# Spreading a per-token factor over all partitions: through DRAM, or with a product of ones on the matmul engine

## The chip, the cores and the metric

One core of a Trainium2 chip runs the whole program in one launch. The engines work in order, each through its own list of instructions, and wait for one another by semaphores: PE multiplies matrices (PEld is its weight load), DVE and ACT work on vectors, POOL does a little, and SP issues all transfers between DRAM and the on-chip memory. On-chip memory has 128 partitions; results of PE land in banks of a second memory (PSUM) of 128 partitions by 512 words. The metric is the device time of one execution in microseconds (us), lower is better.

## The reference, cut to what matters

```python
def rmsnorm(x, w):                       # x: (1, 512, 1024)
    xf = x.astype(jnp.float32)
    y = xf * lax.rsqrt(jnp.mean(xf * xf, axis=-1, keepdims=True) + EPS)
    return (y * w.astype(jnp.float32)).astype(x.dtype)

def hybrid_layer(x, layer_idx, norm_w, w_in, ...):
    h = rmsnorm(x, norm_w)
    proj = jnp.einsum('bsd,de->bse', h, w_in)      # 1024 -> 4608 columns
    aq, ak, av, ag, bq, bk, bv, bg, cu, cg = jnp.split(proj, splits, axis=-1)
    ...                                            # attention, retention, pooling, gates
    mixed = jnp.concatenate([o_a, o_b, o_c], axis=-1)
    return x + jnp.einsum('bse,ed->bsd', mixed, w_out)

def reference(...):                                # two layers, then a last rmsnorm
    h = x
    for l in range(DEPTH):
        h = hybrid_layer(h, l, ...)
    return rmsnorm(h, final_norm_w)
```

512 tokens of 1024 values pass through two layers. The factor of this text is the `lax.rsqrt(...)` of the first rmsnorm: one number for each token, 512 in all.

## The kernel before, in words

All matrices are float32. Each is split into a high and a low half that PE can multiply (`split`, line 449: ACT writes the high half, DVE the rest), and a product of two such matrices is three products (`mm3`, line 495): high by high, high by low, low by high. Names: hh and hl are the halves of the normalised input, stored transposed (channels on partitions); wh and wl those of a block of weights, 128x1024 words, 512 KB, loaded into wraw. Five pairs wh/wl exist and two buffers wraw, so a load may start when both halves of the block two places earlier have been written. In this text the blocks are numbered from 0: blocks 0 to 3 are the value columns bv, block 4 is cg0, block 5 cu0, block 6 cu1.

In the first layer the input arrives transposed from the host. hh and hl there hold x times the norm's weight without the factor of its token, so that PE need not wait for the factors, and each result is multiplied by the factors afterwards. Where tokens lie on partitions (the values, `store_values`, line 739) the factor of a partition is enough: it stands in the four columns `self.rc` (part of the tile edge, 128x4; column t holds tokens 128t to 128t+127). Where tokens lie along the free axis (gates, pooling, rotated q and k), every partition needs all 512 factors in a row: `self.rb`, 128x512. DVE multiplies with it (`scaled_T` line 748, `c_pool` line 906, the tables cos and sin line 777).

The step R of START (lines 730 to 733) makes rb from rc through DRAM: it writes the four columns as a row of 512 words, each word apart, and reads that row back into all 128 partitions.

```python
row = nc.tile("dram", "row", [S], 4, F32)
nc.sync.dma_start(row.rearrange("(t p) -> p t", t=NT), self.rc)
nc.sync.dma_start(self.rb, row.partition_broadcast(P))
```

The order of instructions isn't that of the code. A recorder takes down all operations; a planner (`Recorder.schedule`, line 220) then goes through them with its own model of costs and latencies (`cost`, line 323, and LATENCY) and priorities (place in the program less a boost by kind, HIGH), and writes one list for each engine. Tiles of one tag share a few buffers, granted in the order in which the program names them: 4 of "soft" (128x512), 4 of "T", 1 of "u", 2 banks "tp", 3 banks "pj". Units follow ORDERS: for layer 0 "bv t0 t1 cg0 cu0 cu1 bg0 bg1 bqk0 B0 ..."; t0 (`decay_tables`, line 580) makes small tables out of a load of 8x2 words, in a buffer "soft", by a chain of tiny DVE steps and one exponential on ACT.

Of the kernel before, what the change touches and what calls it, by code (L numbers as in the profile page):

```python
# [9 lines left out]
F32 = mybir.dt.float32  # L10
F32R = mybir.dt.float32r
AF = mybir.ActivationFunctionType
ALU = mybir.AluOpType
AX = mybir.AxisListType

P = 128
S = 512
D = 1024
KD = D // P
NT = S // P  # L20
# [7 lines left out]
UW = PADL + S + 8  # L28
# [341 lines left out]
def record(ins: dict, out: bass.AP):  # L370
    nc = Recorder()
    x_d = ins["x"][0]

    def sb(tag, shape, bufs=1, dt=F32, name=None):
        return nc.tile("sb", tag, shape, bufs, dt)

    def bank(tag, bufs):
        return nc.tile("psum", tag, [P, S], bufs, F32)

    def pj():  # L380
        return bank("pj", 3)

    def lgp():
        return bank("lg", 2)

    def tpp():
        return bank("tp", 2)

    def ovp():
        return bank("ov", 1)  # L390

    def soft():
        return sb("soft", [P, S], 4)

    def ttile(shape=(P, 1024), dt=F32):
        return sb("T", shape, 4, dt)
# [12 lines left out]
    def load_x(t):  # L409
        for half in range(2):  # L410
            nc.sync.dma_start(xt[t][half], x_d[t * P:(t + 1) * P, HALF[half]])
# [2 lines left out]
    nc.vector.memset(neghalf, -0.5)  # L414
    nc.scalar.copy(sb("st", [P, 4], 4), neghalf)
    ident = sb("ident", [P, P])


    granules = [(i, shape) for i, (_, _, _, shape) in enumerate(weight_granules())]
# [3 lines left out]
    def emit_granule(parts=1):  # L423
        at, (nk, nc_) = granules[len(wt)]
        shp = [P, nk, nc_]
        src = ins["wg"][at].rearrange("p (k c) -> p k c", k=nk)
        raw = sb("wraw", shp, 2)
        hi = sb("wh", shp, WBUFS, F32R)
        lo = sb("wl", shp, WBUFS, F32R)
        n = shp[1] // parts  # L430
        for i in range(parts):
            k = slice(i * n, (i + 1) * n)
            was, nc.boost = nc.boost, HIGH.get("w", 0)
            nc.sync.dma_start(raw[:, k, :], src[:, k, :])
            split(hi[:, k, :], lo[:, k, :], raw[:, k, :])
            nc.boost = was
        wt.append((hi, lo))
# [11 lines left out]
    def split(dh, dl, src):  # L449
        nc.scalar.copy(dh, src)  # L450
        nc.vector.tensor_tensor(dl, src, dh.bitcast(F32), op=ALU.subtract)
# [3 lines left out]
    def square(t, half, junk, part=None):  # L455

        if half == 0:
            stats[t] = sb("st", [P, 4], 4)
        st = stats[t]
        c = slice(0, 512) if part is None else part  # L460
        at = half if c.stop == 512 else 3
        nc.scalar.activation(junk, xt[t][half][:, c], AF.Square, scale=1.0 / math.sqrt(D), accum_out=st[:, at:at + 1])
        if half == 0:
            nc.vector.tensor_scalar(st[:, 0:1], st[:, 0:1], EPS, None, op0=ALU.add)
        elif c.stop < 512:
            nc.vector.tensor_tensor(st[:, 0:1], st[:, 0:1], st[:, 3:4], op=ALU.add)
        else:
            nc.vector.tensor_scalar(st[:, 1:2], st[:, 1:2], st[:, 0:1], None, op0=ALU.add)
            nc.gpsimd.tensor_tensor(st[:, 2:3], st[:, 1:2], neghalf[:, 0:1], op=ALU.pow)
# [25 lines left out]
    def mm3(ps, lh, ll, rh, rl, first, last):  # L495
        nc.tensor.matmul(ps, lh, rh, start=first, stop=False)
        nc.tensor.matmul(ps, lh, rl, start=False, stop=False)
        nc.tensor.matmul(ps, ll, rh, start=False, stop=last)
# [180 lines left out]
    class Layer:  # L679
# [18 lines left out]
        def first_values(self):  # L698

            self.vh, self.vl = sb("vh", [P, NT, 512], 1, F32R), sb("vl", [P, NT, 512], 1, F32R)  # L700
            self.rb, self.rc = sb("rb", [P, S]), edge[:, 28:32]

            dummy = sb("soft", [P, S], 4, mybir.dt.bfloat16)
            nc.vector.memset(dummy, 0.0)
            warm = tpp()
            for _ in range(WARM):
                nc.tensor.matmul(warm[:, 0:256], dummy[:, 0:P], dummy[:, 0:256], start=True, stop=True)
            banks = [lgp(), lgp(), ovp(), pj()]
            for u in START.split():
                i = int(u[1:] or 0)  # L710
                if u[0] == "k":
                    xw = ttile()
                    nc.sync.dma_start(xw[:, 0:S + 4], ins["xT_w"][i * P:(i + 1) * P, :])
                    raw, w = xw[:, 0:S], xw[:, S:S + 1]
                    nc.scalar.activation(self.hh[:, i, :], raw, AF.Copy, scale=w)
                    nc.vector.scalar_tensor_tensor(self.hl[:, i, :], raw, w, self.hh[:, i, :].bitcast(F32), op0=ALU.mult, op1=ALU.subtract)
                    if i % 2 == 0:
                        emit_granule(2 if i < FINE else 1)
                    wh, wl = wt[i // 2]
                    for t in range(NT):  # L720
                        ts = slice(t * P, (t + 1) * P)
                        mm3(banks[t], self.hh[:, i, ts], self.hl[:, i, ts], wh[:, i % 2, :], wl[:, i % 2, :], i == 0, i == KD - 1)
                elif u[0] == "x":
                    load_x(i)
                    for half in range(2):
                        square(i, half, soft())
                    nc.vector.tensor_copy(self.rc[:, i:i + 1], stats[i][:, 2:3])
                elif u[0] == "I":
                    nc.sync.dma_start(ident, ins["c_ident"])
                elif u[0] == "R":  # L730
                    row = nc.tile("dram", "row", [S], 4, F32)
                    nc.sync.dma_start(row.rearrange("(t p) -> p t", t=NT), self.rc)
                    nc.sync.dma_start(self.rb, row.partition_broadcast(P))
                else:
                    for t in range(NT):
                        self.store_values(t, banks[t])
            wstate[0] = 4
# [291 lines left out]
@with_exitstack  # L1029
def trunk(ctx: ExitStack, tc: tile.TileContext, ins: dict, out: bass.AP):  # L1030
    pools = {
        "sb": ctx.enter_context(tc.tile_pool(name="sb", bufs=1)),
        "psum": ctx.enter_context(tc.tile_pool(name="ps", bufs=1, space=bass.MemoryType.PSUM)),
        "dram": ctx.enter_context(tc.tile_pool(name="dr", bufs=1, space=bass.MemoryType.DRAM)),
    }
    with tc.manual_schedule():
        for op in record(ins, out).schedule():
            for b in op.bases:
                if b.real is None:
                    name = f"{b.tag}_{b.slot}"  # L1040
                    b.real = pools[b.space].tile(b.shape, b.dt, tag=name, bufs=1, name=name)

            def real(v):
                return v.resolve() if isinstance(v, View) else v

            name, method = op.method
            op.inst = getattr(getattr(tc.nc, name), method)(*[real(a) for a in op.args], **{k: real(v) for k, v in op.kw.items()})  # L1047
# [67 lines left out]
```

## Time and profile before

| | |
|---|---|
| runs, us | 682.93, 682.99, 681.54; median 682.93 |
| profiled execution | 682.16 us, its span 680.4 us |
| busy share | PE 97%, PEld 80%, DVE 74%, ACT 52%, POOL 4% |
| DMA | 71.86 MB, mean 106 GB/s |
| first real product of PE | at 4.78 us, behind the cast of a weight block |
| granted clock, 30 to 55 us in steps of 5 | 1.00, 0.63, 0.50, 0.85, 1.00 |

Times in the profile count from the span's start. A row of a timeline is an instruction or several alike, with its start, its duration, and in brackets the idle time of its engine before it and what ended that. SPq is SP's queue of transfers; its rows show when a transfer is issued, not when it has landed. PEclk is the clock that PE was granted, 1.00 for 2.4 GHz and 0.50 for 1.2 GHz. Matmuls overlap, so the time of one in a stream is the distance of two starts, not the duration shown. All the kernel's own instructions carry line 1047, from where they are issued; the tile names tell them apart.

### The profile page before, as it was taken

The page shows a single profiled execution, that of the slowest core. Times are in us where ns is not written, and L with a number is a line of the kernel's source. Part 1 is how long each engine was busy: PE and PEld are TensorE (multiplying, and loading weights), DVE is VectorE, ACT ScalarE, POOL GpSimd, SP SyncE. Part 2 cuts the span into 40 slices and gives each one's busy share as a digit, 9 for nine tenths or more (in the row PEclk, how much of TensorE's full clock was granted, in tenths as well). Part 3 has the DMA queues.
Part 4 walks back from the last instruction along what each step waited for, and adds up shares of the span by engine and source line. Part 5 has one row for each costly group of instructions (what it writes and reads, how often), then busy time and mean ns, then how long its engine had stood idle before and what let it go on. Part 6 is the DMA issues. An engine that isn't in the chain of part 4 may idle for free. (4 is left out here: it accounts for less than half of the span.)

```text
span 680.4 us, 8912 instructions
## 1 busy us (share of the span) xinstructions
PE 660.3 (97%) x3171; PEld 541.3 (80%) x3171; DVE 500.3 (74%) x954; ACT 354.0 (52%) x701; POOL 30.3 (4%) x51
## 2 busy tenths in 40 slices
PE   9959999999999999999999999899999999999996
PEld 6747887888788888887888888688888887888785
DVE  4558988787787998976574778767568857887733
ACT  6524683534376866553443766344437765665321
POOL 0000000000000000001010000000000000000011
PEclk9969999999999999999999999999999999999999
DMA  8436434422225223243312423532331143124302
GB/s 309 163 123 187 141 93 125 124 93 78 87 61 171 77 91 104 72 116 95 107 63 78 139 68 85 139 109 73 104 118 59 62 137 107 61 92 97 92 31 93
DMA packets 29973, 71.86 MB, mean 106 GB/s; under 512 B 6004, under 2 KB 10260, under 8 KB 29928
## 3 DMA queue, kind: packets, MB, share of 16 engines
q1 hardware_dynamic: 29928, 71.29, 34.4%
q8 instruction: 25, 0.41, 0.3%
q14 instruction: 20, 0.16, 0.1%
HBM read 69.09 MB, written 2.18 MB: 105 GB/s over the span
## 5 line engine op out<-in xcount | busy, mean ns | idle before, releaser
L1047 PE MATMUL pj<-hh,wh 128*128 128x512 f32 x448 | 178.5, 400 | 8.7 <-ACT wh L1047 7.2
L1047 PE MATMUL pj<-hl,wh 128*128 128x512 f32 x448 | 177.8, 397 | 0.0
L1047 PE MATMUL pj<-hh,wl 128*128 128x512 f32 x448 | 177.2, 397 | 0.0
L1047 ACT CAST wh<-wraw 128x1024 fp32r<-128x1024 f32 (+1 forms) x97 | 100.8, 1039 | 108.5 <-PE pj L1047 73.9
L1047 DVE TENSOR_TENSOR wl<-wraw,wh 128x1024 fp32r<-128x1024 f32 (+1 forms) x97 | 117.3, 1209 | 28.5 <-ACT wh L1047 28.0
L1047 PEld LDWEIGHTS pj<-hh,wh 128*128 128x128 f32 x448 | 84.9, 190 | 27.8 <-ACT wh L1047 7.6
L1047 PEld LDWEIGHTS pj<-hh,wl 128*128 128x128 f32 x448 | 84.8, 189 | 18.7
L1047 PEld LDWEIGHTS pj<-hl,wh 128*128 128x128 f32 x448 | 84.8, 189 | 17.8
L1047 PE MATMUL pj<-wh,mAC 128*128 128x512 f32 (+1 forms) x264 | 87.9, 392 | 0.4 <-ACT mAC L1047 0.2
L1047 ACT ACTIVATE soft<-soft,sm 128x512 f32<-128x512 f32 x96 | 67.8, 718 | 33.7 <-DVE sm L1047 33.2
L1047 DVE TENSOR_TENSOR x<-x,pj 128x512 f32<-128x512 f32 (+1 forms) x65 | 43.5, 675 | 23.3 <-PE pj L1047 22.7
L1047 PEld LDWEIGHTS pj<-wh,mAC 128*128 128x128 f32 x264 | 48.9, 188 | 11.4 <-ACT mAC L1047 0.6
L1047 PE MATMUL lg<-qk 128*128 128x512 f32 (+1 forms) x192 | 51.3, 361 | 1.6 <-DVE soft L1047 1.6
L1047 PE MATMUL pj<-wl,mAC 128*128 128x512 f32 (+1 forms) x132 | 51.4, 389 | 0.0
L1047 POOL TENSOR_TENSOR st<-st,neghalf 128x4 f32<-128x4 f32 (+1 forms) x28 | 25.1, 897 | 477.4 <-DVE st L1047 379.3
L1047 DVE CUSTOM_DVE_ANT_0 soft<-lg,wide 128x512 f32<-128x512 f32 x64 | 43.2, 685 | 2.0 <-PE tp L1047 0.4
L1047 PE MATMUL pj<-wh,mB 128*128 128x512 f32 (+1 forms) x136 | 44.5, 383 | 0.0
L1047 PE MATMUL pj<-wh,hl 128*128 128x512 f32 x104 | 41.4, 398 | 0.0
L1047 PE MATMUL pj<-wh,hh 128*128 128x512 f32 x104 | 41.3, 397 | 0.0
L1047 PE MATMUL pj<-wl,hh 128*128 128x512 f32 x104 | 41.2, 396 | 0.0
L1047 PEld LDWEIGHTS lg<-qk 128*128 128x128 f32 x192 | 32.5, 188 | 9.6 <-DVE soft L1047 2.6
L1047 PE MATMUL ov<-T,vh 128*128 128x256 f32 x192 | 39.1, 283 | 0.4 <-DVE og L1047 0.3
(151 smaller groups left out, 948.7 us busy)
## 6 DMA issues: line engine op xcount, KB each, us to landing
wraw<-in_wg SPq DMA_DIRECT2D x95, 512.0 KB, 3.9
hn<-row SPq DMA_DIRECT2D x16, 256.0 KB, 3.9
wide<-gd SPq DMA_DIRECT2D x8, 448.0 KB, 3.8
T<-in_xT_w SPq DMA_DIRECT2D x8, 258.0 KB, 4.6
x<-in_x SPq DMA_DIRECT2D x8, 256.0 KB, 4.8
wide<-dd SPq DMA_DIRECT2D x8, 256.0 KB, 4.8
out<-T SPq DMA_DIRECT2D x8, 256.0 KB, 2.1
qd<-dd SPq DMA_DIRECT2D x8, 128.0 KB
```

Of the source, the lines that this page charges most:

```text
L1047: op.inst = getattr(getattr(tc.nc, name), method)(*[real(a) for a in op.args], **{k: real(v) for k, v in op.kw.items()})
```

## The change

The step R makes rb on the chip. DVE multiplies the 128x128 identity by each of the four columns of rc, which gives four diagonal matrices side by side (dg, 128x512). They are split into a high and a low half (dh, dl). PE multiplies each by a 128x128 matrix of ones, both into one bank: every row of the result is the sum over a diagonal matrix's rows, so the 512 factors in a row. ACT copies the bank to rb. The ones are made at the start, in the buffer "u" by way of one of "T".

```diff
     ident = sb("ident", [P, P])
+    ones = sb("u", [P, UW], 1, F32R)[:, 0:P]
+    onesf = sb("T", [P, 1024], 4)[:, 0:P]
+    nc.vector.memset(onesf, 1.0)
+    nc.vector.tensor_copy(ones, onesf)
...
                 elif u[0] == "R":
-                    row = nc.tile("dram", "row", [S], 4, F32)
-                    nc.sync.dma_start(row.rearrange("(t p) -> p t", t=NT), self.rc)
-                    nc.sync.dma_start(self.rb, row.partition_broadcast(P))
+
+                    dg, dh, dl = soft(), sb("soft", [P, S], 4, F32R), sb("soft", [P, S], 4, F32R)
+                    for t in range(NT):
+                        nc.vector.tensor_scalar(dg[:, t * P:(t + 1) * P], ident, self.rc[:, t:t + 1], None, op0=ALU.mult)
+                    split(dh, dl, dg)
+                    ps = tpp()
+                    nc.tensor.matmul(ps, ones, dh, start=True, stop=False)
+                    nc.tensor.matmul(ps, ones, dl, start=False, stop=True)
+                    nc.scalar.copy(self.rb, ps)
```

The planner's lists change with it. The numbers behind tile names only tell tiles apart; they are about ten higher after the change, and the line 1047 has become 1057.

SP's list, from block 5 of the weights (wraw_276, after the change wraw_277) on; before:

```order
L1047 DMA wraw_276<-in_wg 128x1024
L1047 DMA soft_287<-in_decay 8x2
L1047 DMA row_319<-edge_112 128x4x1
L1047 DMA rb_339<-row_319 128x512
L1047 DMA wraw_348<-in_wg 128x1024
L1047 DMA wraw_397<-in_wg 128x1024
```

and after the change:

```order
L1057 DMA wraw_277<-in_wg 128x1024
L1057 DMA soft_312<-in_decay 8x2
L1057 DMA wraw_345<-in_wg 128x1024
L1057 DMA wraw_413<-in_wg 128x1024
L1057 DMA wraw_423<-in_wg 128x1024
```

The two transfers of the row are gone; block 6 (wraw_348, now wraw_345) follows the decay load.

DVE's list, from the low half of block 4 (wl_327, after the change wl_331) to the first use of rb, in cos; vl is the low half of the values, soft_287 and soft_312 the buffer of the decay tables; before:

```order
L1047 TENSOR_TENSOR wl_327<-wraw_262,wh_315 128x1024
L1047 TENSOR_SCALAR soft_287<-soft_287 8x2 x2
L1047 TENSOR_TENSOR soft_287<-soft_287 8x2
L1047 SCALAR_TENSOR_TENSOR vl_344<-lg_119,edge_112,vh_325 128x512
L1047 TENSOR_SCALAR soft_287<-soft_287 8x2
L1047 SCALAR_TENSOR_TENSOR vl_344<-lg_121,edge_112,vh_325 128x512
L1047 RECIPROCAL soft_287<-soft_287 8x2
L1047 SCALAR_TENSOR_TENSOR vl_344<-ov_125,edge_112,vh_325 128x512
L1047 TENSOR_TENSOR soft_287<-soft_287 8x2
L1047 SCALAR_TENSOR_TENSOR vl_344<-pj_128,edge_112,vh_325 128x512
L1047 TENSOR_TENSOR soft_287<-soft_287 8x2
L1047 TENSOR_TENSOR cos_176<-cos_176,rb_339 128x512
```

and after the change, where soft_289 is dg, soft_329 dh and soft_350 dl:

```order
L1057 TENSOR_TENSOR wl_331<-wraw_263,wh_320 128x1024
L1057 TENSOR_SCALAR soft_312<-soft_312 8x2 x2
L1057 TENSOR_TENSOR soft_312<-soft_312 8x2
L1057 TENSOR_TENSOR soft_350<-soft_289,soft_329 128x512
L1057 TENSOR_SCALAR soft_312<-soft_312 8x2
L1057 SCALAR_TENSOR_TENSOR vl_358<-lg_120,edge_113,vh_335 128x512
L1057 RECIPROCAL soft_312<-soft_312 8x2
L1057 SCALAR_TENSOR_TENSOR vl_358<-lg_122,edge_113,vh_335 128x512
L1057 TENSOR_TENSOR soft_312<-soft_312 8x2
L1057 SCALAR_TENSOR_TENSOR vl_358<-ov_126,edge_113,vh_335 128x512
L1057 TENSOR_TENSOR soft_312<-soft_312 8x2
L1057 TENSOR_TENSOR cos_177<-cos_177,rb_377 128x512
```

dl has come in between the first decay steps and the values, and the fourth vl (from the bank pj) now stands behind cos and sin. In both lists sin follows cos, and the low half of block 5 comes next, after the change with that fourth vl in front of it.

PE's list behind the last value product: before, block 4 (wh_315, wl_327) runs through from its first matmul. After the change (block 4 is wh_320, wl_331; soft_329 is dh, soft_350 dl, u_75 the ones):

```order
L1057 MATMUL tp_342<-soft_329,u_75 128x512
L1057 MATMUL pj_348<-hh_105,wh_320 128x512
L1057 MATMUL pj_348<-hl_111,wh_320 128x512
L1057 MATMUL pj_348<-hh_105,wl_331 128x512
L1057 MATMUL pj_348<-hh_105,wh_320 128x512
L1057 MATMUL pj_348<-hl_111,wh_320 128x512
L1057 MATMUL tp_342<-soft_350,u_75 128x512
L1057 MATMUL pj_348<-hh_105,wl_331 128x512
```

The first product of the ones stands ahead of block 4, the second behind five of its 24 matmuls. Blocks 5 and 6 begin with two matmuls each (high half of the weights), then those with block 5's wl, in both lists.

## Rows read from the trace of the kernel before

**Rows 1.** The page: busy time of PE (share, instructions), clock in 40 slices

```profile
PE 660.3 (97%) x3171; PEld 541.3 (80%) x3171; DVE 500.3 (74%) x954; ACT 354.0 (52%) x701; POOL 30.3 (4%) x51
...
PEclk9969999999999999999999999999999999999999
```

**Rows 2.** Waits of PE, whole span: us in total, times, longest

```profile
PE pj L1047 <- ACT wh L1047: 7.2, 1, 7.2
...
PE pj L1047 <- DVE gate L1047: 1.5, 1, 1.5
```

**Rows 3.** Timeline of PE, 27.8 to 46.8 us: start, duration, instruction, idle before

```profile
27.88 0.40 PE L1047 MATMUL pj<-hh,wh 128*128 128x512 f32 x1
...
33.71 0.39 PE L1047 MATMUL pj<-hl,wh 128*128 128x512 f32 x1
41.32 0.80 PE L1047 MATMUL pj<-hh,wh 128*128 128x512 f32 x1 [7.22 <-ACT wh L1047]
...
46.56 0.40 PE L1047 MATMUL pj<-hh,wh 128*128 128x512 f32 x1
```

**Rows 4.** Windows: length, busy time by engine, PEclk, DMA share, GB/s

```profile
40.00:45.00 5.00, 3.68 (x9) 2.94 (x10) 4.86 (x14) 1.68 (x2) 0.00 (x0) 0.50 0.48 124
50.00:100.00 50.00, 50.00 (x238) 40.93 (x237) 42.84 (x69) 31.64 (x54) 1.30 (x5) 1.00 0.46 133
```

**Rows 5.** Timeline of SP's transfer queue, 21 to 36 us (issue times)

```profile
21.56 0.30 SPq L1047 DMA_DIRECT2D soft<-in_decay  x1
25.06 0.39 SPq L1047 DMA_DIRECT2D row<-edge  x1
35.30 0.34 SPq L1047 DMA_DIRECT2D rb<-row  x1
35.74 0.37 SPq L1047 DMA_DIRECT2D wraw<-in_wg  x1
```

**Rows 6.** Timeline of DVE, 25 to 42 us

```profile
25.50 1.23 DVE L1047 TENSOR_TENSOR wl<-wraw,wh 128x1024 fp32r<-128x1024 f32 x1 [0.47 <-ACT wh L1047]
26.64 0.22 DVE L1047 TENSOR_SCALAR soft<-soft 8x2 f32<-8x2 f32 x2
...
26.91 0.73 DVE L1047 SCALAR_TENSOR_TENSOR vl<-lg,edge,vh 128x512 fp32r<-128x512 f32 x1
...
39.07 0.69 DVE L1047 TENSOR_TENSOR cos<-cos,rb 128x512 f32<-128x512 f32 x1 [8.56 <-DMA rb<-row]
...
39.75 0.67 DVE L1047 TENSOR_TENSOR sin<-sin,rb 128x512 f32<-128x512 f32 x1
...
40.42 1.20 DVE L1047 TENSOR_TENSOR wl<-wraw,wh 128x1024 fp32r<-128x1024 f32 x1
```

**Rows 7.** Timeline of ACT, 23 to 41 us

```profile
23.24 0.63 ACT L1047 ACTIVATE soft<-x 128x512 f32<-128x512 f32 x1 [0.45 <-DMA x<-in_x]
...
27.98 0.18 ACT L1047 ACTIVATE soft<-soft 8x2 f32<-8x2 f32 x1
...
28.66 1.04 ACT L1047 CAST wh<-wraw 128x1024 fp32r<-128x1024 f32 x1
...
40.22 1.04 ACT L1047 CAST wh<-wraw 128x1024 fp32r<-128x1024 f32 x1 [10.52 <-DMA wraw<-in_wg]
```

**Rows 8.** Groups by shape: count, busy us, mean ns of one, idle before

```profile
L1047 ACT COPY hn<-ov 128x512 f32<-128x512 f32 x16 | 9.4, 586 | 16.1 <-DVE og L1047 11.0 <-PE ov L1047 4.0 <-DVE mAC L1047 0.9
...
L1047 DVE TENSOR_SCALAR T<-soft,st 128x512 f32<-128x512 f32 x3 | 1.4, 483 | 1.6 <-POOL st L1047 1.6
```

**Rows 9.** The page's DMA issues: count, KB each, median us to landing

```profile
row<-st SPq DMA_DIRECT2D x16, 2.0 KB, 2.0
```

**Rows 10.** Timeline of DVE and PE, 78 to 110 us

```profile
78.83 0.69 DVE L1047 TENSOR_TENSOR soft<-soft,soft 128x512 f32<-128x512 f32 x1
...
79.84 0.60 PE L1047 MATMUL tp<-ident,soft 128*128 128x128 f32 x4
...
109.68 0.39 PE L1047 MATMUL lg<-vh,T 128*128 128x256 f32 x1 [0.95 <-ACT T L1047]
```

## The prediction

> **What bounds the kernel now.** I read the page's busy table first, then the list of what the matmul engine (PE) waits for, then the timelines of PE, of the DMA queue on SP, of VectorE (DVE) and of ScalarE (ACT) around the one long wait, and the granted clock there. PE is busy for 97% of the span, and the clock row has one weak slice, the third, 34 to 51 us [rows 1]. One wait of PE stands out, 7.2 us for a high half of a weight block (wh); no other single one is above 1.5 [rows 2]. So this is a PE kernel with one hole, and an edit elsewhere counts only where it makes PE late.
>
> The hole: PE starts a 128x512 matmul at 33.71 and the next at 41.32 [rows 3]. SP issues the write of the row (row<-edge) at 25.06; the read-back (rb<-row) waits for that write to land and goes out at 35.30; the next weight blocks stand behind both in the same queue and go out from 35.74 [rows 5]. DVE stands for 8.56 us in front of cos<-cos,rb, and behind that instruction, until 40.42, waits the low half (wl) of block 5, whose high half was cast by 28.66 + 1.04 = 29.70 [rows 6, 7]. So both things that PE needs to go on, wh of block 6 (cast on ACT at 40.22) and wl of block 5, hang on that round trip through memory. The clock falls with it: the granted mean is 0.50 in 40 to 45, the lower level, 1.2 GHz [rows 4], and the old spacing of starts is back only at 46.56.
>
> **The change, part by part.** Durations are those of the profiled execution: 682.16 us, the span 680.4 and 1.76 around it. It lies between the lowest run shown (681.54) and the median (682.93), 0.77 under the median.
>
> (1) The hole goes. Spacing at full clock: (33.71 - 27.88)/25 = 0.233 us. Idle: 41.32 - 33.71 - 0.233 = 7.38. Slow matmuls: 41.32 to 46.56 holds 12 starts, 5.24 - 12 x 0.233 = 2.44 [rows 3]. Together 9.82 us, if nothing else holds PE there.
>
> (2) Added on PE: two 128x512 products, both on the path. No row shows a product with the ones. Below, the spacing of its neighbours of that shape: 2 x 0.233 = 0.47. Above, their spacing at half clock, 5.24/12 = 0.437: 0.87. I take 0.47, since the clock is full at 27.9.
>
> (3) What is late next? The first product goes where block 4 (cg0) now begins, at 27.88. PE then comes to block 6's wh, and to the bank that the fourth value block frees, at 27.88 + (2+24+2) x 0.233 = 34.40, and to block 5's wl at 34.87.
> - wh of block 6: its buffer is free when DVE has written wl of block 4, 25.50 + 1.23 = 26.73. From issue to cast took 40.22 - 35.74 = 4.48 and the cast 1.04 [rows 5 to 7]: 26.8 + 4.5 + 1.0 = 32.3. Spare 2.1.
> - rb: ACT casts dh behind block 4, 25.5 to 26.1 (by the 0.59 of a copy of that shape [rows 8]); two vh, the exponential, two more vh and wh of block 5 follow, to 29.9. dl (0.69 like cos, the same shape) is done on DVE at 26.91 + 0.69 = 27.6 [rows 6]; the second product starts at 27.88 + 6 x 0.233 = 29.28 and is through by 29.7. The copy out of the bank starts when ACT is free and takes 0.59: rb at 30.5.
> - wl of block 5: the exponential, behind dh now, is answered at about 27.7; three vl with a tiny step each, 0.73 apiece, to 29.9; then DVE stands for rb; cos at 30.6, sin 31.3, the fourth vl 31.9, wl 32.7 to 33.9 (0.68, 0.67, 0.73 and 1.2). Spare 1.0. The bank is read by 32.7, spare 1.7.
> No wait, then, but DVE carries dl and the wait for rb in front of that wl, and 1.0 us is all the cover: beyond it, each us costs PE one.
>
> (4) The diagonal: four products of the identity with a column, 128x128 on DVE. No row has that shape. Below: 0.11, half of the row at 26.64 (8x2, two in 0.22) [rows 6]; above: 0.483 (128x512) [rows 8]. I take 0.2, a quarter of the way in columns as in time. Three lie in idle time before the last column is there. The fourth starts in the 0.47 us in which DVE waits for block 4's wh, and even at the upper price it ends with it, 25.03 + 0.48 = 25.51 [rows 6]: 0 either way, for the wl behind it and for dh on ACT. Memset and copy for the ones lie ahead of PE's first weight product, which waits for a cast: 0. Nothing is gained here, since no instruction of DVE goes.
>
> (5) The decay load. It takes a "soft" buffer, and dg, dh and dl now stand ahead of it for one: it gets that of the last squared half-tile (ACT, 23.24 + 0.63, the accumulator read just after), so it is issued at 24.0 where it went at 21.56. DVE reads it at 26.64, ahead of dl. Its duration is not shown, but bounded here: at most 26.64 - 21.56 = 5.1. Among other small transfers the bounds are 2.0 (row<-st) and 35.30 - 25.06 = 10.2 (row<-edge) [rows 5, 6, 9]. From 24.0 it lands at 26.0, 29.1 or 34.2. I take the first: its 8 pieces are nearer to the 128 of row<-st than to the 512 single words of row<-edge. At 29.1, dl is 2.5 late, PE stands for 0.9 at the second product and up to 0.8 more for the wl.
> The Trainium skill (DMA: Bandwidth & Descriptors, section "Anatomy of one DMA — SWDGE (gpsimd) path") gives one transfer about 2.0 us fixed, plus its bytes by the rate. The trace agrees for row<-st (2.0) and not for row<-edge (10.2). By the rule the decay load costs 0 here; by row<-edge it would be case C.
>
> (6) Order behind the hole. The planner reshuffles PE's rows up to some 150 us. The only wait of PE there, 0.95 us at 109.68, could go: -1.0. On the other side, the transposes of the first rotated k start 0.3 us behind the sum that feeds them (79.84 against 78.83 + 0.69) [rows 10]; they now have 2 matmuls of the next block ahead of them, where there were 6: 4 x 0.233 = 0.9 nearer. The logits behind them move as much, 0.9, and the state products trade places with the values', 1.0. So -1.0 to +2.8. I take +0.4, nearer to none, since DVE still idles for 7.2 of the 50 us from 50 to 100 and PE for none of them [rows 4].
>
> Sum: -9.82 + 0.47 + 0.4 = -8.95. That is 673.2 from the profiled execution and 674.0 from the median; I say 673.5.
>
> **The rivals.**
> A. Another wait takes the hole's place: wl of block 5 comes late, through the decay load at its own bound or rb's copy behind a cast. For: 1.0 us of cover, two engines that work in order. Against: every step has a row. Price 1.7 to 3: 675 to 676.5.
> B. The new order makes the first B heads late by the whole 2.8 of (6): 673.5 + 2.4 = 675.9.
> C. Slower than before: the decay load behaves like row<-edge. It stands in front of dl on DVE, and dl in front of PE's second product. Landing at 34.2 puts dl at 35.2, PE idle from 29.3 to 35.3, 6.0, and the clock loss of (1) comes back, 2.44: 673.2 + 8.4 = 681.6, within. It decides from a landing at 36.5, 12.5 us after issue: 2.3 more, 683.9, slower. Against: it took at most 5.1 here.
> D. It doesn't do what it says: the weights are late for another reason and PE stands till about 40: 681 to 683. Against: block 4's buffer is free at 26.73 and nothing but the round trip holds SP.
>
> **How the numbers follow.** Forecast 0.70, its own range 672.0 to 675.0 (the order from -1.0 to +1.0, on either base time). A 0.14, B 0.09, D 0.04, C 0.03. The range, 671.8 to 676.6, takes in A and B. A measurement of this kernel tells 0.2%, 1.4 us, from no change. Faster: forecast, A and B, 0.93; within: D, 0.04; slower: C, 0.03.
>
> **What the profile would show.** Right: no PE wait above 1 us between 25 and 60; the third slice of the clock row at 9; block 6 issued near 26.8; ACT's copy to rb ending near 30.5, cos near 30.6; PE's first use of block 5's wl near 34.9. Wrong at (3): a PE wait at 34 to 35. At (5): DVE idle before the 8x2 work at 26.7 and PE idle at 29.3. At (6): PE waiting for DVE or ACT between 65 and 110. A time above 677 with the hole closed would make the prediction wrong, and the list of PE's waits would have to name the place.

## The result, and the profile after

| | before | after |
|---|---|---|
| median, us | 682.83 (681.54 to 682.99, 4 runs) | 672.72 (672.51 to 673.45, 4 runs) |
| ratio after/before | | 0.9858, 95% interval 0.9841 to 0.9875 |
| profiled execution, its span | 682.16, 680.4 | 673.45, 671.7 |

The change makes the kernel 10.1 us (1.4%) faster by the medians. 673.5 was forecast; the measured time lies 0.8 under that and inside the likeliest case's own range. The two profiled executions differ by 8.7 us, less than the medians, since the one of after is the slowest of its four.

The page's busy table, clock and the head of PE's list of waits (us in total, times, longest) answer to [rows 1, 2]:

```profile
PE 658.1 (98%) x3173; PEld 539.7 (80%) x3173; DVE 502.8 (75%) x961; ACT 355.1 (53%) x703; POOL 30.3 (5%) x51
...
PEclk9999999999999999999999999999999999999999
```

```profile
PE lg L1057 <- DVE soft L1057: 1.6, 2, 1.4
PE tp L1057 <- DVE soft L1057: 1.4, 1, 1.4
PE pj L1057 <- ACT mAC L1057: 1.1, 1, 1.1
```

The wait of 7.2 for wh is gone and no other of its size came instead. The weak slice of the clock row, the third, is gone with it. PE has two instructions more and is busy for 2.2 us less, since the twelve slow matmuls are fast again.

The timeline of PE at the old hole (start, duration, instruction) answers to [rows 3]:

```profile
27.56 0.39 PE L1057 MATMUL tp<-soft,u 128*128 128x512 f32 x1
27.79 0.39 PE L1057 MATMUL pj<-hh,wh 128*128 128x512 f32 x1
...
28.94 0.39 PE L1057 MATMUL tp<-soft,u 128*128 128x512 f32 x1
29.17 0.40 PE L1057 MATMUL pj<-hh,wl 128*128 128x512 f32 x1
...
33.59 0.39 PE L1057 MATMUL pj<-hh,wh 128*128 128x512 f32 x1
33.83 0.39 PE L1057 MATMUL pj<-hl,wh 128*128 128x512 f32 x1
34.05 0.40 PE L1057 MATMUL pj<-hh,wh 128*128 128x512 f32 x1
34.29 0.39 PE L1057 MATMUL pj<-hl,wh 128*128 128x512 f32 x1
34.52 0.39 PE L1057 MATMUL pj<-hh,wl 128*128 128x512 f32 x1
```

The two products with the ones (the rows that read u) stand in the 0.23 spacing of their neighbours. Block 6's first matmul (34.05) and the first use of block 5's wl (34.52) come with no idle time. Their operands are seen on SP, DVE and ACT (the timelines that answer to [rows 5], [rows 6] and [rows 7]):

```profile
24.33 0.29 SPq L1057 DMA_DIRECT2D soft<-in_decay  x1
27.10 8.06 SPq L1057 DMA_DIRECT2D wraw<-in_wg  x3
```

```profile
25.48 0.29 DVE L1057 TENSOR_SCALAR soft<-ident,edge 128x128 f32<-128x128 f32 x1
25.84 1.23 DVE L1057 TENSOR_TENSOR wl<-wraw,wh 128x1024 fp32r<-128x1024 f32 x1
26.98 0.22 DVE L1057 TENSOR_SCALAR soft<-soft 8x2 f32<-8x2 f32 x2
27.17 0.15 DVE L1057 TENSOR_TENSOR soft<-soft 8x2 f32<-8x2 f32 x1
27.25 0.67 DVE L1057 TENSOR_TENSOR soft<-soft,soft 128x512 fp32r<-128x512 f32 x1
...
30.31 0.69 DVE L1057 TENSOR_TENSOR cos<-cos,rb 128x512 f32<-128x512 f32 x1
...
32.39 1.21 DVE L1057 TENSOR_TENSOR wl<-wraw,wh 128x1024 fp32r<-128x1024 f32 x1
```

```profile
29.71 0.57 ACT L1057 COPY rb<-tp 128x512 f32<-128x512 f32 x1
30.36 1.06 ACT L1057 CAST wh<-wraw 128x1024 fp32r<-128x1024 f32 x1
```

Block 6's load went out at 27.10 where it went at 35.74; its cast ended at 31.42, 2.6 before PE needs it. rb was there at 30.28, and block 5's wl ended at 33.60, 0.9 before its use.

### The profile page after: what moved, and what is told of

Its sections match the earlier page's. It is cut to its first block, busy times and chain, and to the rows that moved or that the text cites. A ratio compares the mean times of both kernels' runs of the same rounds, so it can differ in the third digit from the quotient of the medians.

```text
span 671.7 us, 8925 instructions
## 1 busy us (share of the span) xinstructions
PE 658.1 (98%) x3173; PEld 539.7 (80%) x3173; DVE 502.8 (75%) x961; ACT 355.1 (53%) x703; POOL 30.3 (5%) x51
```

## The experiments

The result alone doesn't say why the row's trip through memory took 10.2 us, nor whether it hurt only through the instructions that stood in order behind it, as the prediction had it. **The theory at first** (order): the late weights and cos stand behind the read-back in the lists of SP and DVE; move them and the hole goes, trip or no trip. **The rival** (transfer): the write itself is the trouble, wherever the others stand.

**Order alone.** Three kernels move instructions of the kernel before and change none. `sp_leg` moves the read-back behind block 6's load on SP, `dve_leg` moves cos and sin behind block 5's wl on DVE, `both_legs` does both. The core of the edit on SP, the rest left out:

```diff
...
+        ops.remove(sp[read])
+        ops.insert(ops.index(sp[read + 1]) + 1, sp[read])
...
```

> The kernel before with one instruction moved: on SP the read-back of the row stands behind the load of block 6. DVE's list is as before. Theory (two legs, each holds PE by itself): wh of block 6 is there by 32.3, but DVE still stands in front of cos until about 39, wl of block 5 is written at 41.6, PE stops four matmuls in instead of two: 682 to 683, no change. Rival (SP's queue alone is the cause): the hole closes, 673.

> The kernel before with two instructions moved: on DVE cos and sin stand behind wl of block 5. SP's list is as before. Theory (two legs): wl of block 5 is written by 31.6, but wh of block 6 still comes at 41.3 and PE stops at the same place: 682 to 683. Rival (DVE's stop alone is the cause): the hole closes, 673.

> Both moves together, the slow trip kept. Theory: PE runs through block 5 to about 39.5 and then waits for wl of block 6, which stands behind cos and sin until 41.6: a wait of 2.1 where there were 7.4, and the clock stays up: 682.8 - 9.8 + 2.1 = 675.1, 1 to 2 more if the clock falls all the same. Rival (the legs add up, half each): 673 if each alone gave half.

Measured: `sp_leg` 683.08, ratio 1.0001 (0.9983 to 1.0019); `dve_leg` 683.08, ratio 0.9999 (0.9982 to 1.0015), both times about as expected. In `dve_leg` the path is the expected one too: PE waits 7.02 for wh of block 6, until 40.96. In `sp_leg` it is not. The weights, issued at 27.77 and expected as wh by 32.3, reach their cast only at 38.39, and PE stops first for wh and then for wl:

```profile
39.49 0.79 PE L1053 MATMUL pj<-hh,wh 128*128 128x512 f32 x1 [5.40 <-ACT wh L1053]
42.97 0.80 PE L1053 MATMUL pj<-hh,wl 128*128 128x512 f32 x1 [2.26 <-DVE wl L1053]
```

`both_legs` 679.85, ratio 0.9946 (0.9927 to 0.9965), where 675 to 677 was expected: a third of the gain. PE waits 4.98 for wh of block 6, and the timeline on ACT shows what is late (the bracket: idle before, and what ended it):

```profile
37.48 1.04 ACT L1060 CAST wh<-wraw 128x1024 fp32r<-128x1024 f32 x1 [8.28 <-DMA wraw<-in_wg]
```

SP issued that load at 26.48, 1.7 us behind the write and ahead of the read-back, and ACT found the weights 11.0 us later. Before, the same load took 4.48 from issue to cast. So the theory of order fell short.

**A planner that knows.** `told` gives the planner's model the write's real latency, so that it orders everything around it:

```diff
...
-                op.end = bus + 908
+                op.end = bus + 908 + (8200 if id(op) in self.late else 0)
...
```

> The kernel before with one number changed in the planner: the write of the row lands 8.2 us later than it believed. The read-back then stands behind three weight blocks on SP, cos and sin behind three low halves on DVE. Theory (the trip costs nothing by itself, only what waits behind it): no hole, 672.2 to 672.8, as fast as the change without its products. Rival (the trip itself costs its length, since rb is needed at 34): 680 or more.

Measured 680.18, ratio 0.9968 (0.9956 to 0.9981): a miss by 7.4 us or more. The planner put the read-back behind three weight blocks, and the first of these was late all the same, as on SP and ACT:

```profile
26.90 14.04 SPq L1048 DMA_DIRECT2D wraw<-in_wg  x3
```

```profile
38.28 1.05 ACT L1048 CAST wh<-wraw 128x1024 fp32r<-128x1024 f32 x1 [8.87 <-DMA wraw<-in_wg]
```

PE itself waits little for these weights here, 0.48 and 0.53, because its new list has other work in between. What it does wait for is rb. The third load needs a buffer that DVE frees with the low half of the late block (39.36 + 1.23 = 40.59); it goes out at 40.61 and the read-back at 41.03. cos, sin and the first multiplication of a bank by rb follow on DVE, and PE stands until that bank has been read (the rows are SP's and PE's):

```profile
41.03 0.38 SPq L1048 DMA_DIRECT2D rb<-row  x1
```

```profile
50.18 0.76 PE L1048 MATMUL pj<-hh,wh 128*128 128x512 f32 x1 [4.17 <-DVE soft L1048]
```

So the time of the rival (680 or more) came about, through the late weights.

**The layout of the write.** `packed` keeps the trip through DRAM of the kernel before, but each partition writes its four factors side by side (128 pieces of 16 bytes) and ACT puts them in order after the read-back. `words` has the same read-back and ACT copy with the 512 single words of before; its copy doesn't reorder (0.62 us, in `packed` 1.12).

```diff
-                    nc.sync.dma_start(row.rearrange("(t p) -> p t", t=NT), self.rc)
-                    nc.sync.dma_start(self.rb, row.partition_broadcast(P))
+                    nc.sync.dma_start(row.rearrange("(p t) -> p t", t=NT), self.rc)
+                    mixed_up = soft()
+                    nc.sync.dma_start(mixed_up, row.partition_broadcast(P))
+                    nc.scalar.copy(self.rb.rearrange("p (t q) -> p t q", t=NT), mixed_up.rearrange("p (q t) -> p t q", t=NT))
```

> As 'words', but each partition writes its four factors side by side (128 pieces of 16 bytes); ACT's copy puts them in order. Theory: the write lands after about 2 us like row<-st, the read-back is issued at 27.2 and lands by 31, rb stands at 31.7, no hole, and the two products of the change are not there: 672.2 (0.5 under the changed kernel). Rival (any way through DRAM opens the hole): 680 or more. Rival (new lists): the same as 'words'.

> The kernel before, with one step more: the row comes back into a scratch tile and ACT copies it to rb. The row is still written as 512 single words. Its lists are those of the run 'packed', which differs from it in the layout of the write alone. Theory (the single words make the write land after 10 us, and what stands behind it on SP keeps PE idle): write to read-back about 10.2 us, a hole of about 7 us at 34, 683 us. Rival (the planner's new lists are what helps): no hole, about 673.

Measured: `packed` 673.34, ratio 0.9872 (0.9853 to 0.9890); `words` 680.30, ratio 0.9974 (0.9961 to 0.9988), on the same chip. The two traces have the same instructions in the same order on every engine. `words` is 2.7 us under its expectation: its list on DVE has block 5's wl ahead of cos, so PE runs through block 5 and waits 2.09 for block 6's wh, at 41.45, where it waited 7.22. The page's DMA issues give the write's time from issue to landing (last column), of `words` and then of `packed`:

```profile
row<-edge SPq DMA_DIRECT2D x1, 2.0 KB, 10.4
```

```profile
row<-edge SPq DMA_DIRECT2D x1, 2.0 KB, 2.6
```

The same 2 KB take 10.4 us as 512 words and 2.6 as 128 pieces. With the pieces the trip costs nothing that PE feels: no wait in 25 to 60 us. So the trip through DRAM was not what cost time; the way the row was cut was. The two cuts differ in the number of pieces and in their size at once; which of these counts isn't shown.

**The write alone.** `after_words` is the changed kernel with the old write put back; nobody reads it, nobody waits for it, and every other instruction stands in the order of the changed kernel. `after_packed` does the same with pieces of 16 bytes.

```diff
+                    nc.sync.dma_start(nc.tile("dram", "row", [S], 4, F32).rearrange("(t p) -> p t", t=NT), self.rc)
```

> The changed kernel, with the old write of the four columns of factors put back as it was, 512 single words from the partitions to DRAM, in SP's queue ahead of block 6's weight load; nobody reads what it writes and no instruction waits for it. All other instructions stand in the same order on every engine. In the two runs in which the weight load of block 6 was issued 1.3 to 1.7 us behind this write with nothing on SP holding it, its cast still found the weights only some 11 us after the issue. Theory 1 (the write of single words holds up the transfers that are issued behind it, whoever waits for it): block 6's load, issued at about 27, lands at about 37 to 38, its cast ends at about 39, TensorE stands some 4 to 5 us at block 6's first matmul that was at 34.05, and the time is 677 to 680. Theory 2, the prediction's (only what waits in order behind the slow write is late, and here nothing does): no wait at block 6, 672.5 to 673.3.

> The control to the run with the 512 single words: the same unread write in the same place of SP's queue, but each partition writes its four factors side by side (128 pieces of 16 bytes). Theory 1 (the pieces are what costs) and theory 2 (an unread write costs nothing): both 672.5 to 673.5, no wait of TensorE above 2 us anywhere. A third one (any write to DRAM at this place delays the loads behind it): the same hole as with single words, 677 to 680.

Measured on one chip: `after_words` 680.02, ratio 0.9979 (0.9964 to 0.9994); `after_packed` 674.71, ratio 0.9894 (0.9875 to 0.9913), some 1.2 above its expectation on a chip where the kernel before was at 682.20. The unread words bring the hole back. From the first product of the ones to the heads' first transposes PE takes 27.46 us in the changed kernel (27.56 to 55.02), 27.46 in `after_packed` (27.18 to 54.64) and 34.52 in `after_words` (27.21 to 61.73). So the 1.2 of `after_packed` doesn't come from this place; where it comes from is open. `after_words` on SP, ACT and PE:

```profile
25.46 0.39 SPq L1057 DMA_DIRECT2D row<-edge  x1
27.07 13.61 SPq L1057 DMA_DIRECT2D wraw<-in_wg  x3
```

```profile
38.02 1.04 ACT L1057 CAST wh<-wraw 128x1024 fp32r<-128x1024 f32 x1 [7.76 <-DMA wraw<-in_wg]
```

```profile
39.12 0.79 PE L1057 MATMUL pj<-hh,wh 128*128 128x512 f32 x1 [5.25 <-ACT wh L1057]
```

The windows of 25 to 35 us (length, busy time by engine, clock, DMA share, GB/s), of `after_words` and then of `after_packed`:

```profile
25.00:30.00 5.00, 5.00 (x24) 4.06 (x23) 4.62 (x13) 4.94 (x9) 0.39 (x3) 1.00 1.03 30
30.00:35.00 5.00, 3.87 (x17) 2.80 (x15) 3.51 (x10) 0.26 (x1) 0.00 (x0) 1.00 0.68 29
```

```profile
25.00:30.00 5.00, 5.00 (x24) 4.06 (x23) 4.77 (x14) 4.94 (x9) 0.23 (x3) 1.00 0.42 106
30.00:35.00 5.00, 5.00 (x23) 4.07 (x22) 4.86 (x11) 1.15 (x2) 0.00 (x0) 1.00 0.12 28
```

With the words the DMA engines count as wholly busy while they move 30 GB/s: the weights' packets count as under way and hardly move. The page's DMA issues give the words 11.3 us from issue to landing, so they land at 36.8 (25.46 + 11.3), and the cast finds the weights at 38.02.

**Another queue.** `other_queue` has the same unread words, issued by ACT, so that SP's queue holds only the weights.

```diff
...
+            name, method = ("scalar", "dma_start") if op is words else op.method
```

> The kernel of the run with the unread 512 single words, but the write is issued by ScalarE instead of SP, so that SP's own queue holds the weight loads and nothing else. It costs ScalarE some 0.4 us of issuing (SP's row of that write), which its slack at block 5 bears. In the run with the words on SP, block 6's load was issued at 27.07 and its cast found the weights only at 38.02; the DMA share was 1.03 in 25 to 30 us at 30 GB/s. Theory Q (the words hold up what stands behind them in the same queue): block 6's weights land within 4.5 us of the issue, no wait of TensorE at block 6, 672.5 to 674.7. Theory E (the words occupy the DMA engines, which every queue shares): block 6's weights land at about 37 to 38 again, a wait of 4 to 6 us at block 6, 678 to 681.

Measured 682.45, ratio 0.9975 (0.9963 to 0.9988), that of `after_words`; in us it is above the expected 681, on a chip where the kernel before took 684.28. ACT's timeline:

```profile
24.89 0.40 ACTq L1059 DMA_DIRECT2D row<-edge  x1
...
38.15 1.04 ACT L1059 CAST wh<-wraw 128x1024 fp32r<-128x1024 f32 x1 [7.61 <-DMA wraw<-in_wg]
```

The load went out at 26.83 and was found 11.3 us later, so it isn't the order within one queue. The Trainium skill (DMA: Bandwidth & Descriptors, section "Issuing engines are not separate DMA queues") says that transfers of every issuing engine run on the same 16 DMA engines; this run agrees, with 11.3 from ACT's queue beside 10.95 from SP's. The same page of the Trainium skill, DMA: Bandwidth & Descriptors, says in its section "Specifications" that below 512 bytes a transfer turns into reading, changing and writing back. No run here shows that step, and the 16-byte pieces, also below it, land in 2.6. What in the write of a word takes so long stays open.

**The terms of the sum.** `filled` is the kernel before with block 5's first matmul 31 more times, as much as the idle time holds, so that PE doesn't stop.

```diff
...
+            for _ in range(31 if op is again else 0):
...
```

> The kernel before with block 5's first matmul given 31 times more on PE (its result is overwritten each time), 31 x 0.233 = 7.2 us of work in the hole. Theory (idle time 7.4 us and, apart from it, 2.4 us of matmuls at half clock): the clock stays up, the hole stays as long, 682.8 - 2.4 = 680.4. Rival (the slow matmuls lie beside something else and cost nothing): 682.8.

Measured 681.96, ratio 1.0002 (0.9986 to 1.0018): by the times no gain, and the expected 2.4 us (a ratio of 0.9965) lies outside the interval, which leaves 1.0 at most. In the trace the clock term is there, by the window of 40 to 45 us, where before showed 0.50 [rows 4]:

```profile
40.00:45.00 5.00, 4.75 (x21) 3.53 (x20) 4.86 (x14) 1.73 (x3) 0.00 (x0) 1.00 0.48 121
```

PE reaches the first transposes of the heads 2.3 us earlier than before (62.90 against 65.20), as (1) has it (2.44), but the last norm's only 0.9 earlier (631.74 against 632.66). No single wait accounts for the loss between; the largest that came new is 0.37, at 377.10. So the clock costs PE those 2.4 us at the hole, but what they are worth at the end of the kernel isn't shown.

`products` is the changed kernel with the first product of ones 16 more times.

```diff
...
+            for _ in range(16 if op is again else 0):
...
```

> The changed kernel with the first product of the ones given 16 times more (each overwritten by the next). Theory (a product costs its 0.23 us spacing and lies on the path): 672.7 + 16 x 0.231 = 676.4; rb comes 3.7 later but so does PE's need. Rival (PE has slack there, the products are hidden): 672.7. Upper bound of the prediction (half clock): 679.7.

Measured 675.93, ratio 0.9885 (0.9865 to 0.9905). (675.93 - 672.72)/16 = 0.20 us for one; the two medians were not taken side by side. By the traces, from the first product to the heads' first transposes, it is 31.19 (27.83 to 59.02) against 27.46: 3.73, or 0.233 for each, the spacing.

`late_dl` is the changed kernel with dl computed five times, which tests the cover of (3).

```diff
...
+            for _ in range(4 if op is again else 0):
...
```

> The changed kernel with dl, the low part of the diagonals that the second product of ones needs, computed five times over on VectorE (four extra, 0.6 to 0.67 us each as in its trace, so VectorE's chain behind it is 2.4 to 2.7 us later). It tests the cover that the prediction gave: the second product was 1.0 us behind its operand and block 5's wl ends 0.9 us ahead of its first use. Theory: dl comes 2.4 to 2.7 us later, the cover hides about 1.0, and TensorE waits 1.4 to 1.7 us at the second product or, what is left of it, at block 5's wl: 674.0 to 674.6. Rival (other work hides the rest, or later slack takes it): 672.5 to 673.3. Rival 2 (the delay runs through cos, sin and both wl unhidden): 675 to 675.5.

Measured 674.86, ratio 0.9901 (0.9882 to 0.9921), beside 674.71 of `after_packed` on the same chip: by the times nothing is told apart. The timelines of DVE and PE do tell:

```profile
29.60 0.69 DVE L1062 TENSOR_TENSOR soft<-soft,soft 128x512 fp32r<-128x512 f32 x1
```

```profile
27.85 0.39 PE L1062 MATMUL tp<-soft,u 128*128 128x512 f32 x1
...
30.34 0.50 PE L1062 MATMUL tp<-soft,u 128*128 128x512 f32 x1 [0.96 <-DVE soft L1062]
```

Counted from the first product, dl ended at 0.36 in the changed kernel (27.92 - 27.56) and at 2.44 here (30.29 - 27.85): 2.08 later, of which PE stood 0.96. The cover was 1.1, and what goes beyond it does reach PE at that place; to the heads' first transposes PE takes 28.69 (27.85 to 56.54), 1.23 more than in the changed kernel.

## Why the prediction was right, point by point

- **(1) The hole goes: right.** No wait above 0.1 us from 25 to 60, the clock at 1.00. By two anchors, first and last transposes of the norm in the two traces, PE is 9.74 (93.57 to 83.83) and 9.44 (632.66 to 623.22) earlier. Of both, 0.32 was there already when block 4's turn came (27.88 to 27.56), ahead of the hole; that leaves 9.42 and 9.12, and (1) and (2) give 9.35. The clock's 2.44 is seen at the hole; by `filled` alone it doesn't carry to the end.
- **What held the weights: right in what was named, incomplete in why.** The prediction put the whole delay to order, two legs behind the read-back, and case D was refused because "nothing but the round trip holds SP". `both_legs`, `told`, `after_words` and `other_queue` show a third leg, and `sp_leg` had it already: while the 512 words land, a weight load issued behind them takes 11 us to its cast instead of 4.5, in either queue. Either is enough for a hole: before, the load wasn't issued until the write had landed; in `after_words` it was, and nothing waited. The trace before couldn't show it, since SP issued no load between 25.06 and 35.30 [rows 5]. The forecast held since the change drops the write as well as the waits, and as to this leg that was luck: nothing in the prediction asked for it. Had the change kept the write and moved only the waits, the same reasoning would have been off by 3 to 8 us, as it was for `both_legs`, `told` and, with nothing waiting at all, `after_words`.
- **(2) Two products, 0.47: right.** Spacing 0.23 in the trace, 0.233 each by the traces of `products`.
- **(3) What is late next: right, to 0.35 us but for one.** Forecast and found: block 6's load 26.8 and 27.10, its wh 32.3 and 31.42, rb 30.5 and 30.28, cos 30.6 and 30.31, the end of block 5's wl 33.9 and 33.60, its first use 34.87 and 34.52. The wh, 0.9 early, had been priced at 4.48 from issue to cast and took at most 3.26 (27.10 to 30.36). The cover of 1.0 is 0.9 at the wl and 1.1 at dl by `late_dl`. So A and its price had the right place, and did not occur.
- **(4) The diagonals: the price was low, the cost right.** 0.2 was taken, the groups by shape show 0.284 each, which the bounds held. The fourth ended at 25.77, ahead of the end of block 4's wh (25.81), so it delays nothing:

```profile
L1057 DVE TENSOR_SCALAR soft<-ident,edge 128x128 f32<-128x128 f32 x4 | 1.1, 284 | 0.0
L1057 PE MATMUL tp<-soft,u 128*128 128x512 f32 x2 | 0.8, 394 | 0.0
```

- **(5) The decay load: right.** Issued at 24.33 (24.0 forecast) and read by DVE at 26.98 with no idle time in front, so it took 2.65 at most. It behaved like row<-st [rows 9] and not like row<-edge, and case C with it fell. `packed` and `words` bear out the choice by cut and not by bytes, though not whether the number of pieces or their size decides. The section of the Trainium skill's page DMA: Bandwidth & Descriptors that the prediction names, "Anatomy of one DMA — SWDGE (gpsimd) path", gives its 2.0 us for transfers that GpSimd issues; these go out on SP's queue, where the row of row<-st is what shows 2.0.
- **(6) The order behind the hole: the size was guessed.** The wait that could have gone is still there, 0.8 where 0.95 was [rows 10]; no wait of a k chain came, so B did not occur. By the norm's first transposes (9.42 against 9.35) nothing of the +0.4 shows up to there. In the profiled pair 0.9 us is given back at one place near the end, a wait for a cast of mAC (1.11 at 634.68, 0.19 before). With the same order there it is 1.0 in `after_packed` and `late_dl`, 1.3 in `other_queue`, 0.5 in `after_words` and not seen in `products`. Whether the faster runs of the changed kernel lack it isn't shown, so what makes the gap between 8.7 by the profiles and 10.1 by the medians stays open.

The sum was -8.95 and the medians moved by -10.1, 1.2 us more. The interval of the ratio is a gain of 8.5 to 10.9 us, which holds the sum; the part of it that is a real error of (1) or (6) can't be told from the spread of the runs (681.54 to 682.99 before).

## What to carry to other kernels

A small transfer can be dear by the way it is cut: look at its pieces before its bytes. Here four words side by side did as much, within the intervals, as taking the trip away (`packed` 0.9872, the change 0.9858). A slow write can cost more than the wait for it: here loads issued behind it were held too, in either queue and though nobody waited for it; where a trace shows none behind it, the trace can't tell. So the proof that order is the cause is a kernel with only the order changed, read by its trace too: here `both_legs` fell short in time, and `sp_leg` met its time by another path.

## What had not been expected of the hardware

- 2 KB to DRAM as 512 single words: 10.4 to 12.3 us from issue to landing (`words` 10.4, `other_queue` 12.3); as 128 pieces of 16 bytes 2.6.
- A 512 KB load issued 1.6 to 1.9 us behind those words is found by its cast 10.95 us (`after_words`, 27.07 to 38.02) and 11.3 us (`other_queue`) after its issue, at a DMA share of 1.03 and 30 GB/s. Behind the pieces it is found after 3.8 (`after_packed`, 26.91 to 30.72).
- The write is not seen in the DMA share while it is under way: in the kernel before the windows from 27 to 35 us read 0.00 at 0 GB/s, and the write had landed only when the read-back went out at 35.30 [rows 5].
- An idle of 0.96 us in `late_dl` did not cost PE its clock over the window (granted 1.00 in 30 to 35); the 2.09 and 0.52 of `words` did (0.82 and 0.83 in the two windows from 40 to 50), and so did the 5.25 of `after_words` (0.91 and 0.75 in the two from 35 to 45).
